# Attention and retention branch products of a hybrid encoder layer: half-width order, sums on VectorE, other buffer counts and later planner times

## The chip, the cores and the metric

The kernel runs on one core of one Trainium2 chip. The metric is the device time of one execution in microseconds; the kernel before took 1951.42 us in the median of three runs (1950.37 to 1952.2).

## What is computed

One layer of a streaming encoder, for a prompt of 2048 frames and a sample of 64 frames, in fp32:

```python
h = rmsnorm(x, norm_g) @ w_in                 # 10 groups of columns
qa, ka, va, za, qb, kb, vb, zb, ga, gb = split(h)
oa = diff_attention(qa, ka, va)               # 4 heads of 128
ob = retention(qb, kb, vb)                    # 4 heads of 128
oa = rmsnorm(oa, subln_g) * (1 - lam_init) * silu(za)
ob = rmsnorm(ob) * silu(zb)
m = sigmoid(ga + b_gate[0]) * (oa @ w_oa) + sigmoid(gb + b_gate[1]) * (ob @ w_ob)
y = x + m @ w_out                             # w_oa, w_ob: 512 x 1024, w_out: 1024 x 1024
```

Keys, values and the retention state are outputs too. The change touches the lines from `silu` to `m`, and the loads of the last product.

## The kernel before, in words

Each fp32 operand of a product is split into a high and a low part, and each product is three matmuls (high by high, high by low, low by high). The first and longest part of the program is the input projection (the matmuls of L587) with attention and retention between. Its results, the gates and the branch outputs among them, are kept transposed in DRAM (`zaT`, `zbT`, `gaT`, `gbT`, `oaT`, `obT`). The last two stages are of interest here; they are called the **merge stage** and the **y stage**.

**The merge stage** makes `m`, transposed, in 8 groups of 264 columns (256 prompt frames and 8 sample frames). `out_stream` (L2085) loops over group `g`, branch `br` (0 attention, 1 retention) and 8 column tiles `ct` of 128 channels. `m_tile` (L1797) issues the 12 matmuls of one tile (4 tiles of the contraction by 3, L1816 to L1818) into one PSUM bank. There are eight banks (`mm`, `s` and `at` twice each, `pv`, `tp`), and tile `ct` always gets the same kind of bank, so TensorE can be eight tiles ahead of the bank that has to be emptied next. `m_fin` (L1826) empties it: VectorE multiplies the bank by the gate, in place in the gate's tile (L1831). After branch 0 the result waits in `gm`; after branch 1 GpSimd adds the two (L1842, into a tile `mo`), copies the 8 sample columns aside (L1843, `msf`), and the sum is stored to DRAM (`mT`).

Three chains feed this. `out_prep` (L1709) loads a pair of tiles `on` and `z` (both with tag `oz`, 6 buffers) for each group, branch and half of the contraction; `og_fin` (L1752) multiplies them on GpSimd (L1756), takes the sigmoid of `z` on ScalarE (L1759), multiplies again on VectorE (L1762), and splits the result on ScalarE (L1770, `ogh`) and VectorE (L1773, `ogl`) into tiles with tag `og` (8 buffers: one group). `gate_prep` (L1787) loads the gates in pairs of column tiles, branch 0 into tag `ga` (4 buffers) and branch 1 into tag `gb` (3 buffers), and `gate` (L1778) takes their sigmoid on ScalarE (L1784). `load_wout` (L1642) and `wout_unit` (L1665) prepare `w_out` in the background: loads into `wst` tiles, and work on GpSimd, ScalarE and VectorE (L1669 to L1689).

**The y stage** multiplies `m` by `w_out` with seven block products per group (`y_quad`, L1915; matmuls L1941 to L1943). `y_load` (L1739) loads the four blocks of a group back from `mT` into four `oz` tiles (even groups) or four `ga` tiles (odd ones); `y_sums` and `y_split` (L1854, L1888) form and split the operands.

**What sets the order.** All of these are Python generators run by a planner (`loop`, L92) that keeps a clock for each engine. A step is written out when the planner's TensorE clock has reached the time that the step has asked for. `P`, `A`, `V`, `G` (L125 to L139) charge matmuls, ScalarE, VectorE and GpSimd work; `ld` (L141) issues a load and returns the time at which it is taken to have landed, `nbytes / 300` ns plus `DMA_LAT` (2600 ns); `give(tag, t)` (L122) counts a buffer as free from time `t`, and `take` (L109) waits for that time. The planner's times only set the order of the instructions in each engine's queue. On the chip each engine, and SyncE, which issues every DMA, works its own queue strictly in order, and waits at its head until the semaphores of that instruction have come.

Of the kernel before, what the change touches and what calls it, by code (L numbers as in the profile page):

```python
# [26 lines left out]
GW = 264  # L27
# [39 lines left out]
class Hybrid:  # L67
# [1597 lines left out]
    def wout_unit(self, st, t, dst):  # L1665
        nc = self.nc
        b1, b2, tt = st
        yield t
        nc.gpsimd.tensor_sub(tt[:, 0], b1[:, 1], b1[:, 0])  # L1669
        self.G(256, self.pe)  # L1670
        nc.gpsimd.tensor_sub(tt[:, 1], b2[:, 1], tt[:, 0])
        t1 = self.G(256)
        for d, s in ((dst[0], b1[:, 0:1]), (dst[1], b2[:, 0:1]), (dst[2], tt), (dst[3], b1)):
            n = 256 * s.shape[1]
            if d is dst[2]:
                yield t1
# [5 lines left out]
            nc.scalar.copy(d[0], s)  # L1682
            t = self.A(n, self.pe)
            if d is dst[3]:
                nc.gpsimd.tensor_sub(d[1], s, d[0].bitcast(F32))
                t = self.G(n, t)
            else:
                yield t
                nc.vector.tensor_sub(d[1], s, d[0].bitcast(F32))  # L1689
# [19 lines left out]
    def out_prep(self):  # L1709
        pa = self.z3  # L1710
        for br, name in enumerate(("w_o_diff", "w_o_ret")):
            for kp in range(2):
                h, l = (self.z3w.tile([128, 2, 1024], F32R, tag=f"{name}{n}{kp}", name=f"{name}{n}{kp}") for n in "hl")
                self.wo[br].append((h, l, {}))
        yield from self.load_wo(0)
        for g in range(8):
            gsl = slice(GW * g, GW * g + GW)
            for br, (oT, zT) in enumerate(((self.oaT, self.zaT), (self.obT, self.zbT))):
                for kp in range(2):
                    yield from self.take("oz", 2)  # L1720
# [6 lines left out]
                    self.ogs.append(og)  # L1727
# [6 lines left out]
        yield lambda: all(self.ogs)  # L1734
        for g in range(8):
            yield lambda: len(self.ma) > g
            yield from self.y_sums(g, *self.ma[g])

    def y_load(self):  # L1739
        for g in range(8):  # L1740
            yield lambda: self.mleft[g] == 0 and (self.gated if g % 2 else len(self.ogs) == 32)
            tag, pool = ("ga", self.z4) if g % 2 else ("oz", self.z3)
            yield from self.take(tag, 4)
            a = []
            for ab in range(2):
                for kh in range(2):
                    a.append(self.sb(pool, [128, 2 * GW], tag, "ma")[:, :512])
                    t = self.ld(a[-1].rearrange("p (c t) -> p c t", c=4), self.mT[g, ab, :, 4 * kh:4 * kh + 4, :],
                                1 << 18)
            self.ma.append((a, t, tag))  # L1750

    def og_fin(self, on, z, t, og):  # L1752
        nc = self.nc
        n = 2 * GW
        yield t
        nc.gpsimd.tensor_mul(on, on, z)  # L1756
        t = self.G(n, self.pe)
# [5 lines left out]
        t = self.V(n + 100, t)  # L1763
        self.give("oz", t)
        yield from self.take("og", 2)
# [8 lines left out]
        t = self.V(n + 100, t)  # L1774
        self.give("oz", t)
        og.append((h, l, t))

    def gate(self, g, br, cp, pair):  # L1778
        t = self.ld(pair, (self.gaT, self.gbT)[br][2 * cp:2 * cp + 2, :, GW * g:GW * g + GW]
                    .rearrange("c p n -> p c n"), 270000)  # L1780
        yield t
        for u in range(2):
            ct = 2 * cp + u
            self.nc.scalar.activation(pair[:, u], pair[:, u], AF.Sigmoid, bias=self.bg[:, br, ct:ct + 1])  # L1784
# [11 lines left out]

    def m_tile(self, g, br, ct, og):  # L1797
        nc = self.nc
        csl = slice(128 * ct, 128 * ct + 128)
        tag = ("mm", "s", "at", "mm", "s", "at", "pv", "tp")[ct]  # L1800
        yield from self.take(tag)
        ps = self.psum(tag)[:, :GW]
        for kt in range(4):
# [3 lines left out]
            ready = tw[ct // 2]  # L1807
            if ct == 0 and u == 0:
                k = 4 * g + 2 * br + kp
                yield lambda: len(self.ogs) > k and self.ogs[k]  # L1810
                og.append(self.ogs[k][0])
                ready = max(ready, og[-1][2])
# [6 lines left out]
            for _ in range(3):  # L1819
                t = self.P(GW)  # L1820
        if ct == 7:
            self.give("og", t, 4)
        self.spawn(self.m_fin(g, br, ct, ps, tag, t), 0)
        yield self.pe

    def m_fin(self, g, br, ct, ps, tag, t):  # L1826
        nc = self.nc
# [5 lines left out]
        self.give(tag, t)  # L1833
        if br == 0:
# [5 lines left out]
        yield max(t, t2)  # L1840
        m = self.sb(self.z4, [128, GW], "mo")
        nc.gpsimd.tensor_add(m, a, gs)  # L1842
        nc.gpsimd.tensor_copy(self.msf[:, ct, 8 * g:8 * g + 8], m[:, 256:GW])  # L1843
# [10 lines left out]
    def y_sums(self, g, a, t, tag):  # L1854

# [11 lines left out]
        t3 = self.G(512, t)  # L1867
        self.give(tag, t3)
        yield t
# [7 lines left out]
        t = yield from self.y_split(g, a21)  # L1877
        self.give(tag, t)
        t = yield from self.y_split(g, a12)
        self.give(tag, max(t, t4))  # L1880
        t = yield from self.y_split(g, a22)
        self.give(tag, t)
        if t4 > self.pe:
# [150 lines left out]
    def sample_split(self):  # L2034
        nc = self.nc
        yield lambda: sum(self.mleft) == 0
        yield self.pool + LAT
        h, l = (self.ms[:, :, k] for k in range(2))
        nc.scalar.copy(h, self.msf)
        t = self.A(512, self.pe)  # L2040
        yield t
        nc.vector.tensor_sub(l, self.msf, h.bitcast(F32))
        self.msn.append(self.V(612, t))

    def y_sample(self):
        nc = self.nc
        yield lambda: self.msn and all(len(w) == 4 for w in self.wlast.values())
        yield max(self.msn[0], *(max(w.values()) for w in self.wlast.values()))
        run = []
# [35 lines left out]
    def out_stream(self):  # L2085
        self.spawn(self.gate_prep(), 0)
        self.spawn(self.load_wout(), 2)
        for g in range(8):
            for br in range(2):
                og = []  # L2090
                for ct in range(8):
                    yield from self.m_tile(g, br, ct, og)
        self.z3x.close()
# [75 lines left out]
    def z_stream(self):  # L2169
# [28 lines left out]
        self.z3w = self.z3x.enter_context(self.tc.tile_pool(name="p3w", bufs=1, side="right"))  # L2198
        self.ogs = []
        self.wo = [[], []]  # L2200
        self.spawn(self.out_prep(), 1)

    def run(self):
# [16 lines left out]
        self.gts = {}  # L2220
        self.msn = []
        self.wout_left = 8
# [90 lines left out]
```

## Time and profile before

| what | value |
|---|---|
| median of three runs | 1951.42 us |
| the profiled execution's own time | 1950.76 us |
| its span in the trace | 1948.9 us |
| granted TensorE clock, mean | 0.995 |
| TensorE busy in the span | 1925.5 us |
| VectorE, ScalarE, GpSimd busy | 1085.8, 1005.5, 530.8 us |

Busy times are sums over the instructions of an engine; on TensorE, matmuls overlap, so a window is full when its busy time equals its length. The granted clock is the share of full speed that TensorE was given. "Idle before" is the time an engine stood still ahead of a group of instructions, with what ended it. A wait "A <- B" means that an instruction of A was released last by one of B.

### The profile page before, as it was taken

To read this page: it belongs to the slowest core of one execution; us is meant where nothing else is said; L and a number is where in the kernel's file an instruction comes from. 1 tells how busy PE (TensorE), PEld (TensorE's weight loads), DVE (VectorE), ACT (ScalarE), POOL (GpSimd) and SP (SyncE) were. 2 spreads that over 40 slices of the span, in tenths; PEclk is the share of its full clock that TensorE was granted. 3 is DMA by queue.
4 is the path that set the end of the run, shared out by engine and by line. 5 is a ranking of instruction groups with operands and counts; after the bars stand their busy time and mean duration, and the time that the engine had idled before them with its cause. 6 is when DMAs were issued, how large, how long until landed. Compare 5 with 4: busy or idle time off the path is not lost.

```text
span 1948.9 us, 32905 instructions
## 1 busy us (share of the span) xinstructions
PE 1925.5 (99%) x11614; PEld 1713.8 (88%) x11614; DVE 1085.8 (56%) x2665; ACT 1005.5 (52%) x2137; POOL 530.8 (27%) x493
## 2 busy tenths in 40 slices
PE   9999999999999999999999999999999999989999
PEld 7878899999889999999988888888888899988787
DVE  6553565636545345638746646646653336646664
ACT  6442676645454535536657656645754435543221
POOL 2320121212121223211112121121112538765442
PEclk9999999999999999999999999999999999999999
DMA  7647464336665868554243242453244656677542
GB/s 246 211 141 195 137 173 127 108 94 170 171 178 161 245 185 233 169 177 149 93 133 117 88 137 92 128 167 98 66 122 134 218 170 205 203 240 224 194 156 77
DMA packets 356198, 308.49 MB, mean 158 GB/s; under 512 B 65729, under 2 KB 313537, under 8 KB 356034
## 3 DMA queue, kind: packets, MB, share of 16 engines
q1 hardware_dynamic: 356034, 306.39, 53.2%
q8 instruction: 92, 1.51, 0.3%
q14 instruction: 72, 0.59, 0.1%
HBM read 201.38 MB, written 99.88 MB: 155 GB/s over the span
## 4 chain that ended last, share of the span: by engine, by line
PE 91%; DMA 3%; POOL 3%; DVE 1%; issue 1%; ACT 1%; SPq 0%; POOLq 0%; ACTq 0%; DVEq 0%
PE mm L587 55%; PE s L1061 3%; PE s L1062 3%; PE at L1169 3%; PE pv L1149 2%; PE pv L1148 2%; PE pv L1147 2%; PE s L1941 1%; PE s L1942 1%; PE s L1943 1%; DMA on<-oaT 1%; PE pv L1528 1%; PE at L1518 1%; PE at L1943 1%; PE tp L784 1%
## 5 line engine op out<-in xcount | busy, mean ns | idle before, releaser
L587 PE MATMUL mm<-xh,wh 128*128 128x512 f32 (+2 forms) x1280 | 457.5, 357 | 0.0
L587 PE MATMUL mm<-xh,wl 128*128 128x512 f32 (+2 forms) x1280 | 452.4, 353 | 0.0
L587 PE MATMUL mm<-xl,wh 128*128 128x512 f32 (+2 forms) x1280 | 451.9, 353 | 0.0
L551 POOL TENSOR_TENSOR wl<-ws,wh 128x512 fp32r<-128x512 f32 x189 | 253.8, 1357 | 671.4 <-ACT wh L541 517.3
L587 PEld LDWEIGHTS mm<-xh,wl 128*128 128x128 f32 x1280 | 240.9, 188 | 31.2
L587 PEld LDWEIGHTS mm<-xh,wh 128*128 128x128 f32 x1280 | 241.3, 189 | 29.0
L587 PEld LDWEIGHTS mm<-xl,wh 128*128 128x128 f32 x1280 | 241.3, 189 | 28.8
L587 PE MATMUL mm<-wh,xh 128*128 128x256 f32 (+1 forms) x696 | 235.9, 339 | 0.5 <-ACT raw L749 0.3
L587 PE MATMUL mm<-wh,xl 128*128 128x256 f32 (+1 forms) x696 | 231.2, 332 | 0.0
L587 PE MATMUL mm<-wl,xh 128*128 128x256 f32 (+1 forms) x696 | 230.7, 331 | 0.0
L1184 DVE TENSOR_TENSOR atl<-at,ath 128x512 fp32r<-128x512 f32 (+1 forms) x144 | 93.0, 659 | 146.5 <-ACT ath L1182 146.5
L887 ACT COPY ev<-mm 128x512 f32<-128x512 f32 x140 | 71.4, 510 | 187.1 <-PE mm L587 164.1
L1100 ACT ACTIVATE row<-row,a_mx 128x1024 f32<-128x1024 f32 (+7 forms) x160 | 153.9, 963 | 5.0 <-DVE a_mx L1080 5.0
L1070 DVE CUSTOM_DVE_ANT_0 row<-s,dfar 128x512 f32<-128x512 f32 (+2 forms) x192 | 117.9, 630 | 58.5 <-PE s L1062 58.2
L587 PEld LDWEIGHTS mm<-wh,xh 128*128 128x128 f32 x696 | 131.9, 190 | 14.1 <-ACT raw L749 0.8
L587 PEld LDWEIGHTS mm<-wh,xl 128*128 128x128 f32 x696 | 131.8, 189 | 13.3
L587 PEld LDWEIGHTS mm<-wl,xh 128*128 128x128 f32 x696 | 132.0, 190 | 12.8
L541 ACT CAST wh<-ws 128x512 fp32r<-128x512 f32 x192 | 115.2, 617 | 47.3 <-PE mm L587 23.5
L950 POOL TENSOR_TENSOR r_y<-r_y,r_sq 128x256 f32<-128x256 f32 x33 | 25.8, 783 | 415.6 <-DVE r_sq L947 143.4
L1182 ACT CAST ath<-at 128x512 fp32r<-128x512 f32 (+1 forms) x144 | 78.5, 565 | 100.0 <-PE at L1169 96.9
L1061 PE MATMUL s<-K,q 128*128 128x512 f32 (+3 forms) x320 | 119.4, 377 | 0.0
L1062 PE MATMUL s<-K,q 128*128 128x512 f32 (+3 forms) x320 | 115.6, 363 | 0.0
(383 smaller groups left out, 4210.6 us busy)
## 6 DMA issues: line engine op xcount, KB each, us to landing
ws<-in_w_in_dram SPq DMA_DIRECT2D x192, 256.0 KB, 3.2
q<-qT SPq DMA_DIRECT2D x128, 128.0 KB, 3.0
V<-vN SPq DMA_DIRECT2D x24, 512.0 KB, 5.6
K<-kT SPq DMA_DIRECT2D x48, 256.0 KB, 4.1
ga<-gaT SPq DMA_DIRECT2D x32, 264.0 KB, 4.1
gb<-gbT SPq DMA_DIRECT2D x32, 264.0 KB, 4.6
xt<-in_x_prompt_dram SPq DMA_DIRECT2D x16, 512.0 KB, 6.0
kn<-in_cache_k_T_dram SPq DMA_DIRECT2D x32, 256.0 KB, 3.4
```

What stands on the lines that cost most here:

```text
L541: self.nc.scalar.copy(h, st)
L551: self.nc.gpsimd.tensor_sub(l, st, h.bitcast(F32))
L587: nc.tensor.matmul(ps, p, q, start=c == 0 and i == 0, stop=c == KC - 1 and i == 2)
L887: nc.scalar.copy(ev, ps)
L1061: nc.tensor.matmul(ps, q1s, kk, start=True, stop=False)
L1062: nc.tensor.matmul(ps, q2s, kk, start=False, stop=True)
L1070: nc.vector.tensor_tensor_reduce(out=units[k0 // 1024][:, k0 % 1024:k0 % 1024 + n], in0=ps, in1=tab, scale=-SLOPES[h], scalar=3.0e38, op0= ...
L1100: nc.scalar.activation(u, u, AF.Exp, bias=mx, scale=-1.0, accum_out=lp[:, k:k + 1])
L1147: nc.tensor.matmul(o, v0, ah[:, s0:s0 + n], start=kt == 0, stop=False)
L1169: nc.tensor.transpose(at[:, w:w + 128], src, self.ident)
L1182: nc.scalar.copy(ah[:, :w], at[:, :w])
L1184: nc.vector.tensor_sub(al[:, :w], at[:, :w], ah[:, :w].bitcast(F32))
```

## The change

- **Half-width order.** A group is now run as four quarters of four column tiles, from a table `HALVES`: for even groups branch 0 on tiles 0 to 3, branch 1 on tiles 0 to 3, branch 1 on tiles 4 to 7, branch 0 on tiles 4 to 7; for odd groups with the branches exchanged. The branch that is first on a half puts its gates into `ga` tiles, the second into `gb` tiles, and the sum is made after the second. The `og` tiles of a branch are given back after its second quarter. Banks go round by a running count, no longer by column tile.
- **Sums on VectorE.** The sum of the branches and the copy of the sample columns move from GpSimd to VectorE.
- **Buffers.** `oz` has 7 tiles instead of 6, `ga` 3 instead of 4. For the y stage an odd group's blocks go to three `ga` tiles and one `gb` tile, each taken by itself, and a group's loads now also wait until two operands of the group ahead are split.
- **Later times in the planner.** A new `LATE` (1000 ns) is added when `oz`, `wst`, `ga`, `gb` tiles are given back and before a sum is stored; a new `LAND` (2000 ns) is added to the time from which loaded `on`, `z` and gate tiles may be used.
- `sample_split` no longer waits for the count of finished sums but uses the time of the last one.

Core of the diff:

```diff
-        "oz": 6, "og": 8, "ga": 4, "gb": 3, "wst": 4, "mo": 4, "xr": 8, "cap": 6}
+        "oz": 7, "og": 8, "ga": 3, "gb": 3, "wst": 4, "mo": 4, "xr": 8, "cap": 6}
...
+LATE = 1000.0
+LAND = 2000.0
...
+HALVES = [[(a, 0, 0), (b, 0, 1), (b, 1, 0), (a, 1, 1)] for a, b in ((0, 1), (1, 0))]
...
-        self.give("wst", t, 3)
+        self.give("wst", t + LATE, 3)
...
-            for br, (oT, zT) in enumerate(((self.oaT, self.zaT), (self.obT, self.zbT))):
+            for br in (0, 1) if g % 2 == 0 else (1, 0):
+                oT, zT = ((self.oaT, self.zaT), (self.obT, self.zbT))[br]
...
     def y_load(self):
         for g in range(8):
...
+            yield lambda: g == 0 or len(self.ya[g - 1]) > 1
+            tags = ("ga", "ga", "ga", "gb") if g % 2 else ("oz",) * 4
...
     def og_fin(self, on, z, t, og):
...
-        yield t
+        yield t + LAND
         nc.gpsimd.tensor_mul(on, on, z)
...
-        self.give("oz", t)
+        self.give("oz", t + LATE)
...
     def gate(self, g, br, cp, pair):
...
-        yield t
+        yield t + LAND
...
     def gate_prep(self):
         for g in range(8):
-            for br in range(2):
-                for cp in range(4):
-                    tag = ("ga", "gb")[br]
+            for br, half, second in HALVES[g % 2]:
+                for cp in range(2 * half, 2 * half + 2):
+                    tag = ("ga", "gb")[second]
                     yield from self.take(tag)
...
-        tag = ("mm", "s", "at", "mm", "s", "at", "pv", "tp")[ct]
+        self.nbank += 1
+        tag = ("mm", "s", "at", "mm", "s", "at", "pv", "tp")[self.nbank % 8]
...
-        nc.gpsimd.tensor_add(m, a, gs)
-        nc.gpsimd.tensor_copy(self.msf[:, ct, 8 * g:8 * g + 8], m[:, 256:GW])
-        t = self.G(GW, t)
-        t2 = self.G(40)
+        nc.vector.tensor_add(m, a, gs)
+        t = self.V(GW, t)
+        nc.vector.tensor_copy(self.msf[:, ct, 8 * g:8 * g + 8], m[:, 256:GW])
+        self.msn = self.V(20)
         if ct % 2:
-            self.give("ga", t + SLACK)
-            self.give("gb", t + SLACK)
-        yield t2 + 2000
+            self.give("ga", t + LATE)
+            self.give("gb", t + LATE)
+        yield t + LATE
...
         for g in range(8):
-            for br in range(2):
-                og = []
-                for ct in range(8):
-                    yield from self.m_tile(g, br, ct, og)
+            ogs = [[], []]
+            for k, (br, half, second) in enumerate(HALVES[g % 2]):
+                for ct in range(4 * half, 4 * half + 4):
+                    yield from self.m_tile(g, br, ct, second, ogs[br])
+                if k > 1:
+                    self.give("og", self.pe + LAT, 4)
```

New lines push the code down: what was L1756, L1831, L1842 and L1843 is L1762, L1835, L1847 and L1849 in the changed kernel, and L1669 to L1685 are L1674 to L1690.

GpSimd's queue in the merge stage before, at the end of group 0: the sums and copies (`mo`, `msf`), the work on `w_out` (`wst`, `wt43l`) and a product for a later group (`on`) stand in one line.

```order
L1842 TENSOR_TENSOR mo<-ga,gb 128x264
L1843 COPY msf<-mo 128x8
L1842 TENSOR_TENSOR mo<-ga,gb 128x264
L1843 COPY msf<-mo 128x8
L1756 TENSOR_TENSOR on<-on,z 128x528
L1678 TENSOR_TENSOR wst<-wst 128x256
L1685 TENSOR_TENSOR wt43l<-wst,wt43h 128x2x256
```

A stretch of the same queue, early in the merge stage of the changed kernel:

```order
L1674 TENSOR_TENSOR wst<-wst 128x256
L1676 TENSOR_TENSOR wst<-wst 128x256
L1685 TENSOR_TENSOR wst<-wst 128x256
L1762 TENSOR_TENSOR on<-on,z 128x528
L1683 TENSOR_TENSOR wst<-wst 128x256
L1690 TENSOR_TENSOR wt43l<-wst,wt43h 128x2x256
```

The sums and copies are gone from this queue; the products `on` now follow only work on `w_out`.

VectorE's queue before, over the second branch of group 0 (products of banks and gates, with work on `w_out` and the low parts `ogl` between):

```order
L1831 TENSOR_TENSOR gb<-mm,gb 128x264
L1773 TENSOR_TENSOR ogl<-on,ogh 128x528
L1689 TENSOR_TENSOR wb21l<-wst,wb21h 128x256
L1831 TENSOR_TENSOR gb<-s,gb 128x264
L1689 TENSOR_TENSOR wt12l<-wst,wt12h 128x2x256
L1831 TENSOR_TENSOR gb<-at,gb 128x264
L1831 TENSOR_TENSOR gb<-mm,gb 128x264
L1831 TENSOR_TENSOR gb<-s,gb 128x264
L1831 TENSOR_TENSOR gb<-at,gb 128x264
L1831 TENSOR_TENSOR gb<-pv,gb 128x264
L1831 TENSOR_TENSOR gb<-tp,gb 128x264
L1762 TENSOR_TENSOR on<-on,z 128x528
```

VectorE's queue in the changed kernel, over the last quarter of group 0:

```order
L1779 TENSOR_TENSOR ogl<-on,ogh 128x528 x2
L1835 TENSOR_TENSOR gb<-at,gb 128x264
L1835 TENSOR_TENSOR gb<-pv,gb 128x264
L1847 TENSOR_TENSOR mo<-ga,gb 128x264
L1849 COPY msf<-mo 128x8
L1847 TENSOR_TENSOR mo<-ga,gb 128x264
L1849 COPY msf<-mo 128x8
L1835 TENSOR_TENSOR gb<-tp,gb 128x264
L1847 TENSOR_TENSOR mo<-ga,gb 128x264
L1849 COPY msf<-mo 128x8
```

Each product of a second branch is now followed, at once or one product later, by its sum and its copy in the same queue.

More of the change, by code (lines that the diff above doesn't have):

```diff
@@ L1733, in out_prep @@
         self.spawn(self.y_load(), 1)
-        yield lambda: all(self.ogs)
+        yield lambda: all(self.ogs.values())
         for g in range(8):
@@ L1740, in y_load @@
         for g in range(8):
-            yield lambda: self.mleft[g] == 0 and (self.gated if g % 2 else len(self.ogs) == 32)
-            tag, pool = ("ga", self.z4) if g % 2 else ("oz", self.z3)
-            yield from self.take(tag, 4)
+            yield lambda: self.mleft[g] == 0 and (self.gated if g % 2 else self.oput == 32)
+            yield lambda: g == 0 or len(self.ya[g - 1]) > 1
+            tags = ("ga", "ga", "ga", "gb") if g % 2 else ("oz",) * 4
             a = []
[L1745 to L1750, printed above, removed]
+            for k, tag in enumerate(tags):
+                yield from self.take(tag)
+                a.append(self.sb(self.z4 if g % 2 else self.z3, [128, 2 * GW], tag, "ma")[:, :512])
+                kh = 4 * (k % 2)
+                t = self.ld(a[-1].rearrange("p (c t) -> p c t", c=4), self.mT[g, k // 2, :, kh:kh + 4, :], 1 << 18)
+            self.ma.append((a, t, tags))
     def og_fin(self, on, z, t, og):
@@ L1774, in og_fin @@
         t = self.V(n + 100, t)
-        self.give("oz", t)
+        self.give("oz", t + LATE)
         og.append((h, l, t))
@@ L1807, in m_tile @@
             ready = tw[ct // 2]
[L1808 to L1811, printed above, removed]
+            if u == 0 and len(og) == kp:
+                yield lambda: self.ogs[g, br, kp]
+                og.append(self.ogs[g, br, kp][0])
                 ready = max(ready, og[-1][2])
@@ L1820, in m_tile, with m_fin @@
                 t = self.P(GW)
-        if ct == 7:
-            self.give("og", t, 4)
-        self.spawn(self.m_fin(g, br, ct, ps, tag, t), 0)
+        self.spawn(self.m_fin(g, br, ct, second, ps, tag, t), 0)
         yield self.pe
-    def m_fin(self, g, br, ct, ps, tag, t):
+    def m_fin(self, g, br, ct, second, ps, tag, t):
         nc = self.nc
@@ L1833, in m_fin @@
         self.give(tag, t)
-        if br == 0:
+        if not second:
             self.gm[ct] = (gs, t)
@@ L1867, in y_sums @@
         t3 = self.G(512, t)
-        self.give(tag, t3)
+        self.give(tags[0], t3)
         yield t
@@ L1877, in y_sums @@
         t = yield from self.y_split(g, a21)
-        self.give(tag, t)
+        self.give(tags[2], t)
         t = yield from self.y_split(g, a12)
-        self.give(tag, max(t, t4))
+        self.give(tags[1], max(t, t4))
         t = yield from self.y_split(g, a22)
-        self.give(tag, t)
+        self.give(tags[3], t)
         if t4 > self.pe:
@@ L2035, in sample_split @@
         nc = self.nc
-        yield lambda: sum(self.mleft) == 0
-        yield self.pool + LAT
         h, l = (self.ms[:, :, k] for k in range(2))
         nc.scalar.copy(h, self.msf)
-        t = self.A(512, self.pe)
+        t = self.A(512, max(self.pe, self.msn))
         yield t
         nc.vector.tensor_sub(l, self.msf, h.bitcast(F32))
-        self.msn.append(self.V(612, t))
+        self.t_ms = self.V(612, t)
     def y_sample(self):
         nc = self.nc
-        yield lambda: self.msn and all(len(w) == 4 for w in self.wlast.values())
-        yield max(self.msn[0], *(max(w.values()) for w in self.wlast.values()))
+        yield lambda: all(len(w) == 4 for w in self.wlast.values())
+        yield max(self.t_ms, *(max(w.values()) for w in self.wlast.values()))
         run = []
@@ L2198, in z_stream @@
         self.z3w = self.z3x.enter_context(self.tc.tile_pool(name="p3w", bufs=1, side="right"))
-        self.ogs = []
+        self.ogs = {(g, br, kp): [] for g in range(8) for br in range(2) for kp in range(2)}
+        self.oput = 0
         self.wo = [[], []]
```

14 lines of the change are left out of this document (8 added, 6 removed).

## The prediction

> **What bounds the kernel now.** First the busy time in windows over the whole span, to find where TensorE is not full.
>
> ```profile
> 0.00:1400.00 1400.00, 1394.37 (x8464) 1242.30 (x8465) 797.67 (x2180) 780.94 (x1690) 271.78 (x223) 1.00 0.53 152
> 1600.00:1650.00 50.00, 45.45 (x350) 45.24 (x349) 29.76 (x54) 24.43 (x53) 37.30 (x46) 0.93 0.72 218
> 1700.00:1750.00 50.00, 45.98 (x354) 45.65 (x353) 24.70 (x46) 20.81 (x44) 31.63 (x43) 0.93 0.78 233
> 1850.00:1900.00 50.00, 50.00 (x217) 40.46 (x216) 31.77 (x42) 12.66 (x21) 21.25 (x13) 1.00 0.46 152
> ```
>
> The columns are the window, its length, the busy time of TensorE, its weight loads, VectorE, ScalarE and GpSimd, the granted clock, the DMA share and GB/s. TensorE is full at full clock outside the merge stage, so only that stage can give much. Next its borders and the length of a tile, from TensorE's timeline (first matmul of the first two tiles, of the last two, and of the y stage), and the stage as one window.
>
> ```profile
> 1571.80 0.28 PE L1816 MATMUL mm<-ogh,w_o_diffh 128*128 128x264 f32 x1
> 1573.25 0.28 PE L1816 MATMUL s<-ogh,w_o_diffh 128*128 128x264 f32 x1
> ...
> 1776.14 0.28 PE L1816 MATMUL pv<-ogh,w_o_reth 128*128 128x264 f32 x1
> ...
> 1777.61 0.28 PE L1816 MATMUL tp<-ogh,w_o_reth 128*128 128x264 f32 x1
> ...
> 1779.09 0.40 PE L1941 MATMUL mm<-wb11h,mh 128*128 128x512 f32 x1
> ...
> 1571.80:1779.10 207.30, 194.80 (x1538) 193.23 (x1537) 113.66 (x203) 98.69 (x212) 136.25 (x177) 0.97 0.70 209
> ```
>
> The stage lasts 207.3 us. A tile that waits for nothing takes 1.45 us (1571.80 to 1573.25) to 1.47 us (1776.14 to 1777.61), and the 128 tiles 185.6 to 188.2 us; I take 187. The stage therefore loses about 20 us: 12.5 us of idle TensorE (207.30 less 194.80), and the rest to a lower clock, 0.97 in the mean (0.03 x 207 is 6 us). Windows of 5 us show where the clock falls.
>
> ```profile
> 1640.00:1645.00 5.00, 1.22 (x5) 1.22 (x6) 4.66 (x8) 5.00 (x12) 3.80 (x5) 0.81 0.84 257
> 1645.00:1650.00 5.00, 5.00 (x25) 5.00 (x24) 1.72 (x5) 1.20 (x3) 4.94 (x6) 0.51 0.43 129
> 1710.00:1715.00 5.00, 2.61 (x12) 2.61 (x13) 3.47 (x8) 3.70 (x8) 3.27 (x5) 0.64 0.96 283
> 1715.00:1720.00 5.00, 5.00 (x31) 5.00 (x31) 1.95 (x3) 2.08 (x4) 4.20 (x7) 0.68 0.95 280
> 1750.00:1755.00 5.00, 3.20 (x27) 2.99 (x26) 2.71 (x4) 3.64 (x8) 3.56 (x4) 1.00 0.25 73
> ```
>
> Then the waits of TensorE, which name what ends them.
>
> ```profile
> PE pv L1816 <- DVE ga L1831: 4.6, 1, 4.6
> PE pv L1816 <- DVE gb L1831: 3.9, 1, 3.9
> ...
> PE tp L1816 <- DVE ga L1831: 1.8, 1, 1.8
> PE mm L1817 <- DVE ogl L1773: 1.1, 1, 1.1
> ...
> PE mm L1816 <- ACT ogh L1770: 1.0, 1, 1.0
> ...
> PE at L1943 <- DVE ml L1896: 0.6, 2, 0.4
> PE at L1941 <- ACT mh L1893: 0.4, 1, 0.4
> ```
>
> Two waits of 4.6 and 3.9 us, and one of 1.8, are for a bank that VectorE has not emptied although TensorE was eight tiles (11.6 us) ahead; 2.1 us are for operands, and 1.0 us falls into the y stage. The two long ones are followed by the slow clock, the 1.8 us one (at 1750) is not. VectorE is not short of time (113.66 of 207.3 us). What held it is seen in the waits of the other engines around the second long stall, in their sums for the stage, and in SyncE's timeline.
>
> ```profile
> ACT z L1759 <- POOL on L1756: 8.5, 2, 7.0
> DVE on L1762 <- ACT z L1759: 7.0, 2, 4.9
> ...
> SPq L142 <- POOL mo L1842: 20.8, 12, 3.7
> SPq L142 <- POOL msf L1843: 16.1, 10, 4.0
> ...
> SPq L142 <- POOL wt43l L1685: 14.3, 4, 6.5
> ...
> 1693.74 10.06 SPq L142 DMA_DIRECT2D wst<-in_w_out_dram  x3
> ```
>
> It is one ring. SyncE stood for most of 10 us at loads of `w_out` tiles that GpSimd had not freed; the loads of `on` and of gates lay behind; GpSimd's next product waited for its load, ScalarE's sigmoid of `z` for GpSimd (7.0 us), VectorE's product for that (4.9 us), and the products that empty the banks stood behind it. The bound of this stage is queues that stand at an instruction written out too early.
>
> **The change, part by part.** The rows with the prices:
>
> ```profile
> ga<-gaT SPq DMA_DIRECT2D x32, 264.0 KB, 4.1
> gb<-gbT SPq DMA_DIRECT2D x32, 264.0 KB, 4.6
> ...
> L1773 DVE TENSOR_TENSOR ogl<-on,ogh 128x528 fp32r<-128x528 f32 x28 | 28.8, 1057 | 2.3 <-ACT ogh L1770 2.3
> L1831 DVE TENSOR_TENSOR ga<-s,ga 128x264 f32<-128x264 f32 x16 | 6.8, 426 | 10.8 <-ACT ga L1784 10.8
> L1689 DVE TENSOR_TENSOR wb21l<-wst,wb21h 128x256 fp32r<-128x256 f32 x8 | 6.1, 764 | 0.5 <-ACT wb21h L1682 0.5
> ...
> L1784 ACT ACTIVATE ga<-ga,bg 128x264 f32<-128x264 f32 x64 | 29.2, 507 | 33.9 <-DMA ga<-gaT 33.9
> ...
> L1770 ACT CAST ogh<-on 128x528 fp32r<-128x528 f32 x28 | 16.3, 625 | 1.8 <-issue 1.8
> ...
> L1842 POOL TENSOR_TENSOR mo<-ga,gb 128x264 f32<-128x264 f32 x57 | 48.7, 855 | 6.4 <-DMA mT<-mo 3.4 <-DVE gb L1831 3.1
> L1843 POOL COPY msf<-mo 128x8 f32<-128x8 f32 x56 | 20.2, 360 | 3.0
> ...
> L245 DVE TENSOR_TENSOR sm_t<-sm_t,ms x51: 155/166/1224, 81.0 to 1489.0; 128x8 f32<-128x8 f32 x32, 128x4 f32<-128x4 f32 x16, 64x8 f32<-64x8 f32 x2, 64x4 f32<-64x4 f32 x1
> ```
>
> *Later planner times.* The planner took a gate pair as landed after 270000/300 + 2600 = 3500 ns; the rows say 4.1 and 4.6 us. With `LAND` it counts 5.5 us, above both medians, so sigmoids and products of `on` stand later in the queues than their data arrive. `LATE` does the same for freed buffers, and so for SyncE. These edits add no instruction. What they cost is lead: about 3 us of the time between a buffer's release and its use.
>
> *Sums off GpSimd.* GpSimd loses 48.7 + 20.2 us of its 136.25 and keeps 67. SyncE's waits for sums and copies (20.8 and 16.1 us) then hang on VectorE. VectorE gains 64 sums and 64 copies. No row has a sum there. From below, a sum costs 0.42 us (the 264-wide product from a bank); from above 0.76 us (the 256-wide difference of two SBUF tiles while GpSimd works); a copy about 0.17 us (the smallest operations). That is 38 to 60 us, or 151 to 173 us busy in a stage of 187. I take the lower half, about 45, since GpSimd does half as much. It lies in VectorE's idle time; if that cover went, each us above 187 would be a us of the stage.
>
> Here the Trainium skill has a rule that speaks against the move: "GPSIMD Engine Reference", section 1 (Specifications), says that GpSimd shares its SBUF interfaces with VectorE and contends with VectorE instructions that have two SBUF inputs. The added sums are of that kind. The rows agree: `ogl` with two SBUF inputs averages 1057 ns, far above twice the 426 ns of the half as wide product from a bank. By the rule all sums would take the upper price; the stage would still fit.
>
> *Half-width order, three `ga` tiles.* A half (two branches on four tiles) is 8 tiles, 11.6 us. With three tiles, the gates of a half's second first-branch pair need the tile of the half before that its second branch frees in its middle. From that release the ring is: SyncE up to 1 us (estimate), landing 4.6, two sigmoids 1.0, two products 0.85, two products of the second branch 0.85, two sums and copies 1.2: 9.5 us. It fits into 11.6 us with 2 us to spare, and eight banks lend another 11.6 us once. Before, the ring with four tiles had a whole group (23.3 us) for about the same work. So this edit frees SBUF for a seventh `oz` tile at the price of a tighter ring. It is the part that I trust least.
>
> *Operands.* A branch's `og` tiles come free a quarter (5.8 us) before the next group needs them, where it was half a group (11.6 us). Two casts and two low parts take 1.25 + 2.1 us by the rows, which fits. I leave the 2.1 us of operand waits in the sum.
>
> *The y stage.* Its products are the same, at the same rate. Only its first operands change place; their tiles come free in the last quarter, 5.8 us ahead, and each product takes longer than its split. I cost it at nothing; the bounds are its 1.0 us of waits gone or doubled.
>
> **Sum.** Against the profiled execution's 1950.76 us: less 20.4 us (207.3 to 187), plus 2.1 us of operand waits, plus 1.8 us for one short bank wait of the kind seen at 1750, gives 1934. Its own time is 0.66 us below the median of the runs shown, so I give 1935. Lower bound: the whole loss goes and tiles run at 1.45 us, 1951.4 less 21.7 (207.3 to 185.6), less 1 us in the y stage: 1929.
>
> For the clock, "TensorE: Matmul & The Clock Gate", part 1, of the Trainium skill says that the clock is halved after an idle window of about 3.4 us and comes back after as much busy time. That agrees with the rows: 0.51 to 0.81 after the long stalls, 1.00 after the 1.8 us one. By the rule two such recoveries cost about 3.4 us together; the windows give 6 to 8, which I use.
>
> **The rivals.**
>
> *Half the stalls stay* (the stage loses 8 to 14 us): the queues still meet transfers that land late, since the landing times are medians and the DMA share reaches 0.95 in the rows around 1715. Against it: GpSimd no longer carries sums, which is the first link of the ring. With 11 of the 20.4 us left the time is 1951.4 less 9.4, 1942.
>
> *The three-tile gate ring paces the stage* (slower). Place: loads of `ga` in the middle of each half. Point: the ring above 11.6 us. Two low parts (2.1 us) queued on VectorE within the ring would bring 9.5 to just 11.6; one late landing on top passes it. Over 16 halves each us above costs 15 us, less the 11.6 us that the banks lend. It turns slower than before at (20.4 + 11.6)/15 = 2.1 us above, 13.7 us; at 14.5 us it gives about 1962. Against it: low parts do not fall into every ring, and VectorE's queue puts the products of the first branch together.
>
> *The stalls only move*: the later planner times stretch the rings as much as they unblock the queues, and the time stays within 0.2% (4 us, about what a measurement of this kernel can tell): 1950.
>
> **How the numbers follow.** The forecast (1929 to 1938) has 0.70. Half the stalls stay: 0.16. The stalls move: 0.05. The gate ring: 0.09. Faster by over 0.2% has 0.86, the same 0.05, slower 0.09. The range reaches from 1929 over the forecast and the second case to 1946.
>
> **What would show it.** Right: the merge stage at 187 to 191 us, granted clock 1.00 throughout it, no wait of TensorE over 2 us, GpSimd near 67 us in the stage and VectorE at 150 to 165, and SyncE's waits for `mo` and `msf` gone or short. Wrong: waits of TensorE's bank for VectorE while VectorE waits for `ga` sigmoids and these for DMA (the gate ring), VectorE above 175 us with sums near 0.76 us, waits on `ogh` at the start of quarters, or a later first product of the y stage.

## The result, and the profile after

The changed kernel takes 1929.8 us (median of four runs, 1929.18 to 1930.79) against 1951.81 us before (four runs, 1950.37 to 1952.23). The ratio is 0.9889, 95% interval 0.9876 to 0.9901: faster by 1.1%, 22 us. The profiled execution took 1930.18 us, with a span of 1928.4 us.

First the borders of the merge stage, from TensorE's timeline, and the stage and two stretches of the y stage as windows (columns as in the prediction's first fence).

```profile
1572.21 0.28 PE L1822 MATMUL s<-ogh,w_o_diffh 128*128 128x264 f32 x1
...
1760.44 0.39 PE L1946 MATMUL mm<-wb11h,mh 128*128 128x512 f32 x1
```

```profile
1572.20:1760.44 188.24, 187.66 (x1537) 187.33 (x1536) 158.22 (x330) 99.72 (x215) 73.77 (x63) 1.00 0.80 237
1760.00:1800.00 40.00, 40.00 (x176) 32.42 (x176) 34.21 (x47) 14.77 (x26) 17.79 (x11) 1.00 0.75 244
1800.00:1900.00 100.00, 100.00 (x431) 80.28 (x430) 59.14 (x78) 24.90 (x42) 40.12 (x26) 1.00 0.46 146
```

The stage lasts 188.2 us, 19.1 less than before. TensorE idles 0.6 us in it instead of 12.5, and the granted clock is 1.00 throughout. The rest, from the first y product to the end of the span, takes 168.0 us (1928.4 less 1760.44) where it took 169.8. The stage began 0.4 us later. Together that is 20.5 us, the difference of the two spans (1948.9 and 1928.4). These are the waits of TensorE and then of SyncE in the stage, and the groups of VectorE and of GpSimd. Line 147 is a load, line 152 a store (142 and 147 before).

```profile
PE at L1823 <- DVE ogl L1779: 0.6, 1, 0.6
```

```profile
SPq L152 <- DVE msf L1849: 41.4, 32, 7.5
SPq L147 <- DVE ogl L1779: 13.0, 13, 3.4
SPq L147 <- DVE mo L1847: 7.9, 7, 2.1
SPq L152 <- DVE mo L1847: 7.7, 10, 1.7
...
SPq L147 <- POOL wt43l L1690: 6.4, 4, 2.2
```

```profile
L1847 DVE TENSOR_TENSOR mo<-ga,gb 128x264 f32<-128x264 f32 x62 | 35.5, 572 | 0.9
L1779 DVE TENSOR_TENSOR ogl<-on,ogh 128x528 fp32r<-128x528 f32 x28 | 22.3, 826 | 0.1
...
L1849 DVE COPY msf<-mo 128x8 f32<-128x8 f32 x62 | 19.9, 320 | 2.1
...
L1762 POOL TENSOR_TENSOR on<-on,z 128x528 f32<-128x528 f32 x22 | 31.6, 1438 | 37.6 <-DMA on<-oaT 13.2 <-DVE ga L1835 10.4 <-DMA on<-obT 8.8
```

No bank wait is left. SyncE still stands, but elsewhere. Before, its loads stood 97.7 us in all, 36.9 of them for GpSimd's sums and copies; now they stand 49.5 us, 7.9 of them for VectorE's sums. Its stores stood 23.6 us and now stand 58.1, 49.1 of them for VectorE's sums and copies. Loads that lie behind a standing store are late by that much, and still TensorE has what it needs: idle time of SyncE shows trouble only when what lies behind it is wanted.

### The profile page after: what moved, and what is told of

Read it like the earlier page. It is cut to its first block, busy times and chain, and to the rows that moved or that the text cites. A ratio compares the mean times of both kernels' runs of the same rounds, so it can differ in the third digit from the quotient of the medians.

```text
span 1928.4 us, 32898 instructions
## 1 busy us (share of the span) xinstructions
PE 1918.3 (99%) x11614; PEld 1708.6 (89%) x11614; DVE 1133.9 (59%) x2793; ACT 1004.4 (52%) x2137; POOL 459.2 (24%) x365
## 4 chain that ended last, share of the span: by engine, by line
PE 95%; DVE 2%; DMA 1%; ACT 1%; issue 0%; POOL 0%; SPq 0%; DVEq 0%; ACTq 0%; POOLq 0%
PE mm L592 55%; PE s L1066 3%; PE s L1067 3%; PE at L1174 3%; PE pv L1154 2%; PE pv L1153 2%; PE pv L1152 2%; PE s L1946 1%; PE s L1948 1%; PE s L1947 1%; PE pv L1533 1%; PE at L1523 1%; PE tp L789 1%; PE at L1946 1%; PE at L1948 1%; PE mm L1946 1%
## 5 line engine op out<-in xcount | busy, mean ns | idle before, releaser
L592 PEld LDWEIGHTS mm<-xl,wh 128*128 128x128 f32 x1280 | 241.3, 189 | 28.7
L1075 DVE CUSTOM_DVE_ANT_0 row<-s,dfar 128x512 f32<-128x512 f32 (+2 forms) x192 | 118.0, 630 | 58.3 <-PE s L1067 58.1
L546 ACT CAST wh<-ws 128x512 fp32r<-128x512 f32 x192 | 115.2, 617 | 49.1 <-PE mm L592 23.1
```

Of the source, the lines that this page charges most:

```text
L546: self.nc.scalar.copy(h, st)
L592: nc.tensor.matmul(ps, p, q, start=c == 0 and i == 0, stop=c == KC - 1 and i == 2)
L1075: nc.vector.tensor_tensor_reduce(out=units[k0 // 1024][:, k0 % 1024:k0 % 1024 + n], in0=ps, in1=tab, scale=-SLOPES[h], scalar=3.0e38, op0= ...
```

## The experiments

Two theories. **Times**: the queues stood because instructions were written out too early, and `LAND` and `LATE` cured that. This is where the prediction put its weight. **Sums**: GpSimd, in whose queue the sums lay among its products, was the link of the ring that could not keep up, and moving the sums cured it. A rival to both is the half-width order, as a gain or as a tight ring. Each part was undone in the changed kernel, and each put alone into the kernel before. Ratios are to the kernel before, timed on the same chip. The stage is from the first `ogh` product to the first y product.

### Sums back on GpSimd

```diff
-        nc.vector.tensor_add(m, a, gs)
-        t = self.V(GW, t)
-        nc.vector.tensor_copy(self.msf[:, ct, 8 * g:8 * g + 8], m[:, 256:GW])
-        self.msn = self.V(20)
+        nc.gpsimd.tensor_add(m, a, gs)
+        t = self.G(GW, t)
+        nc.gpsimd.tensor_copy(self.msf[:, ct, 8 * g:8 * g + 8], m[:, 256:GW])
+        self.msn = self.G(40)
```

> The changed kernel with one part undone: the sums and the copies of the sample columns run on GpSimd again. Theory 1 (planner times: the stalls came from instructions written out before their data had landed) expects little: 1930 to 1935 us, merge stage under 193 us, GpSimd near 140 us busy in it. Theory 2 (GpSimd's queue was the link that closed the ring) expects most of the stalls back: 1942 to 1952 us, with waits of TensorE's banks of 2 us and more. Theory 3 (the half-width order is what gives the room) expects 1930 to 1935 us.

Measured: 1963.97 us, ratio 1.0056 (1.0041 to 1.0071), so slower than the kernel before, and above what any of the three theories gave. The stage lasts 223.5 us. TensorE's waits in the stage, SyncE's, and windows over the longest of them:

```profile
PE mm L1822 <- DVE ga L1835: 27.9, 5, 17.5
```

```profile
SPq L152 <- POOL mo L1847: 61.3, 26, 7.9
SPq L152 <- POOL msf L1849: 48.7, 28, 6.9
```

```profile
1571.40:1794.90 223.50, 194.84 (x1537) 193.51 (x1536) 116.81 (x206) 99.99 (x215) 139.53 (x187) 0.93 0.66 199
1650.00:1655.00 5.00, 0.92 (x8) 0.70 (x6) 3.98 (x5) 1.62 (x5) 4.94 (x6) 1.00 0.52 150
1655.00:1660.00 5.00, 0.00 (x0) 0.00 (x0) 1.25 (x1) 0.48 (x1) 2.62 (x5) 0.54 0.67 193
1660.00:1665.00 5.00, 0.00 (x0) 0.00 (x0) 0.00 (x0) 0.00 (x0) 0.19 (x1) 0.50 1.04 350
```

Between 1660 and 1665 all five engines all but stand, and the DMA is at its peak. The timelines of SyncE, GpSimd, ScalarE, VectorE and TensorE give the chain, in this order:

```profile
1642.86 1.22 SPq L147 DMA_DIRECT2D wst<-in_w_out_dram  x2
1648.98 0.37 SPq L152 DMA_DIRECT2D mT<-mo  x1
...
1653.65 0.36 SPq L152 DMA_DIRECT2D mT<-mo  x1
...
1659.55 0.42 SPq L147 DMA_DIRECT2D on<-oaT  x1
...
1664.81 1.29 POOL L1762 TENSOR_TENSOR on<-on,z 128x528 f32<-128x528 f32 x1 [7.06 <-DMA on<-oaT]
1666.07 0.72 POOL L1683 TENSOR_TENSOR wst<-wst 128x256 f32<-128x256 f32 x1
...
1666.82 0.62 ACT L1687 CAST wt43h<-wst 128x512 fp32r<-128x512 f32 x1 [11.35 <-POOL wst L1683]
1667.35 0.92 ACT L1790 ACTIVATE ga<-ga,bg 128x264 f32<-128x264 f32 x2
...
1667.89 0.43 DVE L1835 TENSOR_TENSOR ga<-mm,ga 128x264 f32<-128x264 f32 x1 [11.14 <-ACT ga L1790]
...
1668.38 0.59 PE L1822 MATMUL mm<-ogh,w_o_reth 128*128 128x264 f32 x1 [17.46 <-DVE ga L1835]
```

SyncE stood from 1644.1 to 1649 and again to 1653.6 at stores of sums that GpSimd had not made. The load of `on` was therefore issued at 1659.55. GpSimd's product waited 7.06 us for it, with a `w_out` difference behind it. ScalarE stood 11.35 us at the cast of that difference, with the gate sigmoid behind it; VectorE 11.14 us at the product that needs this sigmoid; and TensorE 17.46 us for its bank. It is the prediction's ring with all later planner times in place, closed by the sums on GpSimd. One link differs: there SyncE stood at loads of `w_out` tiles, here at stores of sums and copies (110.0 us in the stage, 61.3 and 48.7).

### Planner times undone, one by one

```diff
-LAND = 2000.0
+LAND = 0.0
```

> The changed kernel with LAND set to 0: loads count as landed after 3.5 us again, the rest stays. Theory 1 expects bank waits of TensorE to come back in part: 1935 to 1945 us, with ScalarE waiting for gate loads ahead of other work. Theories 2 and 3 expect no change: 1929 to 1932 us.

Measured: 1931.93 us, ratio 0.9892 (0.9877 to 0.9907), stage 188.9 us. Nothing lost that can be measured. For `LATE`, the `ga` and `gb` tiles again come free at `SLACK` (400), and a sum's store keeps its 1000 ns:

```diff
-LATE = 1000.0
+LATE = 0.0
-            self.give("ga", t + LATE)
-            self.give("gb", t + LATE)
-        yield t + LATE
+            self.give("ga", t + SLACK)
+            self.give("gb", t + SLACK)
+        yield t + 1000.0
```

> The changed kernel with LATE set to 0 (gate tiles given back 400 ns after the sum, as before), LAND and the rest kept. Theory 1 expects SyncE to stand longer at loads whose tile is not free: 1932 to 1940 us. Theories 2 and 3 expect no change: 1929 to 1932 us.

Measured: 1929.85 us, ratio 0.9886 (0.9869 to 0.9902), stage 188.0 us. Nothing either.

### Full-width order kept

```diff
-HALVES = [[(a, 0, 0), (b, 0, 1), (b, 1, 0), (a, 1, 1)] for a, b in ((0, 1), (1, 0))]
+HALVES = [[(0, 0, 0), (0, 1, 0), (1, 0, 1), (1, 1, 1)]] * 2
-        "oz": 7, "og": 8, "ga": 3,
+        "oz": 6, "og": 8, "ga": 4,
```

(The branches are also loaded in their old order, and `og` tiles come free after each branch.)

> The changed kernel with the order undone: each group runs branch 0 on all eight column tiles, then branch 1, with four ga tiles and six oz tiles as before; sums on VectorE, LATE and LAND stay. Theory 1 and theory 2 expect little: 1929 to 1934 us. Theory 3 expects most of the stalls back: 1942 to 1952 us. If the half-width order made the gate ring tighter, as the prediction feared, this one is no slower than the changed kernel.

Measured: 1927.78 us, ratio 0.9873 (0.9856 to 0.9889), stage 187.3 us without any wait of TensorE:

```profile
1571.28:1758.58 187.30, 187.30 (x1538) 187.30 (x1537) 160.22 (x331) 99.98 (x215) 77.55 (x65) 1.00 0.79 240
```

So the half-width order brings nothing here; its interval overlaps that of the whole change, so the 2 us between them are not settled.

### Parts alone

Into the kernel before went `LATE` and `LAND` only:

> The kernel before with the later planner times alone (1000 ns on oz, wst, ga, gb tiles given back, 2000 ns on the landing of on, z and gates); order, buffers and sums on GpSimd as before. Theory 1 expects most of the gain: 1931 to 1938 us. Theory 2 (GpSimd) and theory 3 (order) expect 1945 to 1953 us.

Measured: 1953.55 us, ratio 1.001 (1.0001 to 1.0019). The stage is 212.6 us, with 18.2 us of bank waits. The times alone bring nothing. The sums and copies alone:

> The kernel before with the sums and copies on VectorE alone. Theory 2 expects most of the gain: 1931 to 1938 us. Theories 1 and 3 expect little: 1943 to 1953 us, with VectorE's queue standing at products whose sigmoid is late.

Measured: 1935.5 us, ratio 0.9915 (0.9901 to 0.993), 16.6 us of the gain. The half-width order with seven `oz` and three `ga` tiles, and the changed loads of the y stage, with sums on GpSimd and the early planner times:

> The half-width order, seven oz and three ga tiles alone: sums on GpSimd and early planner times as before. Theory 3 expects most of the gain: 1931 to 1938 us. Theories 1 and 2 expect 1943 us or more; the gate ring that the prediction feared would put it above 1952 us.

Measured: 1963.61 us, ratio 1.0057 (1.004 to 1.0074): some 11 us slower than before. In its stage TensorE waits 9.4 us for `ogh`, 0.9 us for `ogl` and 10.2 us for banks. The stage of these two, as windows:

```profile
1571.07:1766.02 194.95, 190.30 (x1537) 189.65 (x1536) 152.80 (x324) 98.30 (x212) 75.45 (x65) 0.98 0.75 227
```

```profile
1571.62:1793.50 221.88, 201.22 (x1537) 197.83 (x1536) 110.07 (x205) 98.64 (x214) 136.58 (x187) 0.94 0.67 200
```

### Both planner times undone together

Undone one by one they cost nothing, and yet the sums alone (0.9915) stayed 0.26%, 5 us, behind the whole change (0.9889). So both went at once: from the changed kernel, and from the one with the full-width order.

> The changed kernel with both planner times of before (LAND 0, buffers counted free early), so that the sums on VectorE and the half-width order stand alone. Each time alone could be undone at no cost. If one covers for the other: 3 to 8 us lost, 1933 to 1938, with waits of SyncE for buffers and TensorE's waits for banks back. If the times are worth nothing in any combination: 1928 to 1932, and what lies between the sums alone (1935.5) and the whole change comes from the other parts.

> The kernel with the full-width order (four ga tiles, six oz tiles) and the sums on VectorE, without the later planner times: what is left of the change beside the sums is the loads of the y stage one tile at a time and the split of the sample columns. If the planner times bring what the sums alone don't (1935.5): about 1935, with the 4.4 us wait of TensorE for a bank. If the y stage's own edits bring it: 1928 to 1930, and the same stage of 188 us in the merge as the changed kernel only by chance.

Measured: 1936.85 us, ratio 0.9923 (0.9906 to 0.994), with the half-width order; 1936.17 us, 0.9923 (0.9905 to 0.9942), with the full width. Each of the two times covers for the other, and the pair is worth 7 to 10 us once the sums are on VectorE (0.34 and 0.50% by the ratios). The y stage's own edits are in the full-width kernel and don't lower its time. With the full width 4.1 us of short bank waits came back, as expected. With the half width it is waits for operands, which was not expected; TensorE's waits there:

```profile
PE at L1823 <- DVE ogl L1779: 5.5, 4, 3.2
PE s L1823 <- DVE ogl L1779: 0.6, 1, 0.6
```

The eight combinations of the three parts, as ratios:

| sums on | order | early times | later times |
|---|---|---|---|
| GpSimd | full | 1 (before) | 1.001 |
| GpSimd | half | 1.0057 | 1.0056 |
| VectorE | full | 0.9915, 0.9923 | 0.9873 |
| VectorE | half | 0.9923 | 0.9889 |

(The two values are without and with the other edits, of the y stage.) The sums decide, the times add to them, and the half-width order costs 0.5 to 0.6% with the sums on GpSimd and nothing that can be told apart otherwise.

### How near VectorE is to its bound

Each sum is made twice, the second time with the same result:

```diff
         self.msn = self.V(20)
+        nc.vector.tensor_add(m, a, gs)
+        t = self.V(GW, t)
```

> The changed kernel with each of the 64 sums made twice (the second writes the same values), which adds about 37 us to VectorE's 157 us in the merge stage (64 times the 574 ns of a sum in the changed kernel's trace). If VectorE's cover ends at the stage's length, as the prediction said, the stage grows from 188 to about 195 to 200 us: 1936 to 1942 us. If queue order alone counts and the load of VectorE does not, 1930 to 1932 us. If the gate ring is near its limit, the added time in each half passes it and it is 1945 us or more.

Measured: 1945.91 us, ratio 0.9966 (0.9953 to 0.9979); the stage is 203.1 us, VectorE busy 185.8 of it. The time lies in the range that was given to the gate ring, above the 1936 to 1942 us for the length of VectorE's work. The trace speaks for VectorE's work all the same. Here is a window over the long middle of the stage, and VectorE's waits for `ga` sigmoids in the whole of it:

```profile
1591.00:1741.00 150.00, 139.26 (x1102) 137.56 (x1102) 145.53 (x290) 76.66 (x163) 65.17 (x56) 0.98 0.75 227
```

```profile
DVE ga L1835 <- ACT ga L1790: 1.8, 2, 1.0
```

VectorE is 97% busy there and waits only 1.8 us for these sigmoids, which a gate ring would have made late. Windows of 20 us of the changed kernel itself show why so little room was left:

```profile
1591.00:1611.00 20.00, 20.00 (x167) 20.00 (x166) 19.25 (x38) 10.72 (x25) 11.04 (x11) 1.00 0.85 253
...
1651.00:1671.00 20.00, 20.00 (x167) 20.00 (x166) 19.62 (x36) 13.30 (x31) 13.68 (x13) 1.00 0.82 249
...
1731.00:1751.00 20.00, 20.00 (x166) 20.00 (x165) 12.60 (x34) 8.41 (x20) 0.00 (x0) 1.00 0.56 164
```

158 of 188 us sounds like slack, but while `w_out` tiles are being split VectorE is 96 to 99% busy; the slack lies in the first 20 us and in the last 50.

### What it is about GpSimd: its place in the ring, or its load

Only the small copies went back:

```diff
-        nc.vector.tensor_copy(self.msf[:, ct, 8 * g:8 * g + 8], m[:, 256:GW])
-        self.msn = self.V(20)
+        nc.gpsimd.tensor_copy(self.msf[:, ct, 8 * g:8 * g + 8], m[:, 256:GW])
+        self.msn = self.G(40, t)
```

> The changed kernel with only the small copies (8 columns) back on GpSimd, and the sums on VectorE. VectorE loses 60 x 0.325 = 19.5 us, GpSimd gains about 21 us. By the in-order queues: each copy makes GpSimd wait for VectorE's sum ahead of its next product, and mo comes free only after it; that is a part of the old ring, so 3 to 15 us lost, 1932 to 1945, with SyncE's waits for msf by GpSimd and TensorE's waits for banks back. If only the amount of work on each engine counts: no loss, 1927 to 1931, since GpSimd with about 95 us and VectorE with about 138 us are both far from 188.

Measured: 1928.6 us, ratio 0.9881 (0.9866 to 0.9896), stage 187.25 us, no wait of TensorE. The waits of GpSimd, then of SyncE:

```profile
POOL msf L1849 <- DVE mo L1847: 26.1, 11, 8.0
```

```profile
SPq L152 <- DVE mo L1847: 27.4, 18, 7.3
SPq L147 <- POOL wt43l L1690: 18.4, 4, 5.6
```

GpSimd stands 26.1 us for VectorE's sums, up to 8.0 us at a time, and that costs nothing: the stores wait for the sum (`DVE mo`), not for the copy. So the expectation of the in-order theory, 3 to 15 us lost, was wrong. GpSimd standing at these copies did no harm here. The other side of the question was put by work that hangs on nothing (a 160-column tile of its own):

```diff
+        nc.gpsimd.tensor_add(self.gx, self.gx, self.gx)
+        nc.gpsimd.tensor_add(self.gx, self.gx, self.gx)
+        self.G(360)
```

> The changed kernel, and behind every sum GpSimd adds a small tile (128x160) of its own to itself twice. Nobody reads it, it waits for nothing, and no DMA hangs on it: about the busy time that the sums and copies had there, without their place in the ring of buffers. If the sums cost the time because each waited for VectorE's products and SyncE's stores and buffers waited for it (in-order queues): no change beyond 5 us, 1928 to 1935, and GpSimd's waits stay short although it is busy some 130 to 150 us in the stage. If they cost it because GpSimd was too busy (its products of branch tiles late) or because it slows VectorE at the shared SBUF interfaces: VectorE's differences of two SBUF tiles back at about 1017 to 1057 ns, and the time back towards the kernel with the sums on GpSimd, 1945 to 1964.

Measured: 1981.59 us, ratio 1.0149 (1.013 to 1.0168); three of its four runs lie between 1979.67 and 1982.67, the fourth took 8727 us, for which no profile was taken. It is not the experiment that was meant. GpSimd's groups between 1575 and 1661, a window of the same kernel, and SyncE's waits from 1600 to 1662:

```profile
L1849 POOL TENSOR_TENSOR gx<-gx 128x160 f32<-128x160 f32 x64 | 31.2, 488 | 4.7
L1848 POOL TENSOR_TENSOR gx<-gx 128x160 f32<-128x160 f32 x64 | 31.1, 486 | 4.5
L1762 POOL TENSOR_TENSOR on<-on,z 128x528 f32<-128x528 f32 x3 | 3.9, 1302 | 0.0
```

```profile
1620.00:1630.00 10.00, 0.00 (x0) 0.00 (x0) 0.00 (x0) 0.00 (x0) 8.81 (x18) 0.57 0.00 0
```

```profile
SPq L147 <- POOL gx L1848: 25.9, 1, 25.9
SPq L147 <- POOL wst L1683: 17.0, 1, 17.0
```

All 128 additions were done in the first 87 us, when only 12 of the sums behind which they were written had been made. So GpSimd's queue does not keep the order of the program text. The kernel says the same: it fixes the order by hand for TensorE, ScalarE and VectorE alone (`manual_schedule` with `MANUAL`, L2230 and L2247 in the kernel before). The stretch of GpSimd's queue shown under "The change" has L1685 ahead of L1683, which `wout_unit` writes first. What was said of the planner in "The kernel before, in words", that its times set the order in each engine's queue, therefore holds for these three engines and not for GpSimd; nor does that list name SyncE. Why the additions went ahead is not shown; that they wait for nothing is a likely reason. Only three products of `on` got through among them. SyncE stood 25.9 us at a load of a `w_out` tile that GpSimd had not freed, and everything else stood behind that. Around it TensorE's windows are empty and its clock falls to 0.57. It shows that work ahead of GpSimd's products is enough to close the ring, with no link to sums, stores or gates. It says nothing on contention, and since the work was bunched, nothing on how much of the sums' cost was their load and how much their place. It also lays open a third reading: moving the sums to VectorE takes them out of a queue that the planner does not order and puts them into one that it does. No run parts that from the change of engine.

## Why the prediction was right or wrong

**What bounds the kernel: right in place and size, half right in cause.** Of about 20 us lost in the merge stage 19.1 came back, and the ring of SyncE, GpSimd, ScalarE, VectorE was seen again, link by link, when the sums went back. The cause given to it, queues that stand at an instruction written out too early, is only half of it. With the sums on GpSimd later planner times change nothing (1.001, 1.0057 to 1.0056). They add 7 to 10 us only where the sums are on VectorE. The forecast took the whole loss less two small terms, whichever part of the change would bring it back. That its number came out therefore says nothing for the cause that it named, and in this it was lucky. (207.3 less 187 is 20.3 us and not 20.4; nothing hangs on the tenth.)

**Later planner times: a gain, not alone.** The prediction gave them no price of their own and let the parts share the 20.4 us. It did not say that the two times can stand for each other. It also took `LATE` to set SyncE's order, which the kernel does not fix by hand.

**Sums off GpSimd: right, its terms less so.** A sum took 0.572 us in the mean, between the bounds of 0.42 and 0.76, and a copy 0.320 us, where 0.17 was taken. Both means mix two kinds, as VectorE's and then GpSimd's timeline show:

```profile
1642.15 0.98 DVE L1847 TENSOR_TENSOR mo<-ga,gb 128x264 f32<-128x264 f32 x1
...
1643.25 0.42 DVE L1847 TENSOR_TENSOR mo<-ga,gb 128x264 f32<-128x264 f32 x1
```

```profile
1642.11 0.74 POOL L1685 TENSOR_TENSOR wst<-wst 128x256 f32<-128x256 f32 x1
1645.14 1.31 POOL L1762 TENSOR_TENSOR on<-on,z 128x528 f32<-128x528 f32 x1 [2.30 <-DMA on<-oaT]
```

Of the 62 sums in the stage's trace, 37 ran while no GpSimd instruction did and took 0.42 to 0.44 us each; the other 25 overlapped one and took 0.785 us in the mean, up to 1.52. Of the 62 copies, 44 of the 45 that overlapped none took 0.17 us; the 17 others took 0.65 us in the mean. So neither bound is a price for all sums: a sum has the lower one while GpSimd stands and up to three times as much while it works. The products from a bank took 0.41 to 0.43 us either way. This agrees with the rule of the Trainium skill on shared SBUF interfaces ("GPSIMD Engine Reference", section 1, Specifications). The prediction's reading of it, all sums at 0.76 us, does not hold, because GpSimd was busy only 73.8 of 188.2 us. `ogl`, also with two SBUF inputs, fell from 1057 to 826 ns as GpSimd's busy time fell from 136.25 us.

Sums and copies are 55.4 us (35.5 and 19.9), but VectorE's busy time rose by only 44.6 (113.66 to 158.22), the 45 that was taken. Two things make up the difference, each about 5.4 us. The other operations became shorter on balance (`ogl` alone by 6.5 us). And neighbouring instructions overlap more: a window's busy time is not a sum over instructions, though it was called one ahead of the prediction. It counts overlapped time once: VectorE's groups add up to 173.9 us in 158.22 us of busy time (124.0 in 113.66 before). So the 45 came out by luck: the work that was added is 55.4 us. GpSimd was predicted at 67 us and had 73.8. What the prediction missed is that VectorE's cover is not 30 us spread out: in the stretch with the `w_out` splits it is nearly used up, which the doubled sums showed.

**Half-width order: rightly the part trusted least.** The gate ring was reckoned at 9.5 us of 11.6, and it holds with the sums on VectorE, where no bank wait is left. With the sums on GpSimd the kernel with this order is 0.5 to 0.6% slower, as the rival had it. That the three-tile ring does this is not shown. In the chain shown above the late `ga` sigmoid stands behind a cast of a `w_out` tile, and that chain starts at stores of sums; in the run with the order alone 9.4 of 20.5 us of TensorE's waits are for `ogh`, and SyncE stands 78.6 us at stores of GpSimd's sums and copies (18.6 before). The prediction did not state that the cost of the order depends on where the sums are made.

**Operands and the short bank wait:** 2.1 and 1.8 us were kept in the sum; 0.6 and 0 remained. **The y stage** was costed at nothing, within 1 us; the rest of the span became 1.8 us shorter, outside that bound. It is no effect of the edits there: from the first y product to the end of the span the kernel with the times alone, whose y stage is the old one, takes 167.3 us too (1951.0 less 1783.69), and the one with the sums alone 167.4 (1933.4 less 1766.02). The one profile of before, with 1.0 us of waits at the start of that stage, is the exception. These three terms are why 1929.8 lies 5 us below the 1935: 2.7 from the stage (190.9 reckoned, 188.2 measured) and 1.8 from the rest, less 0.4 for its later start, and 1.0 from the offset between profiled run and median, which changed its sign.

**What would show it:** stage and clock came out as said. SyncE's waits for `mo` and `msf` did not go (49.1 us at stores), only the loads' did; a store's wait turned out to be no sign of trouble by itself.

**The rivals.** Half the stalls staying, or only moving, is what the sums alone or the times alone give (1935.5 and 1953.55), not the whole change.

Open stay the load of the sums, their place in GpSimd's queue and the order of that queue against each other, why either planner time covers for the other, and whether the full-width order is faster by 2 us.

## What to carry to other kernels

Ask of each operation in an in-order queue what stands behind it and who waits for its result; here a copy whose result nothing wanted soon stood there for 8 us unharmed, while a sum that stores and buffers hang on did not. Ask also who sets the order of that queue. Undo parts one by one and also together: two edits that each look worthless may cover for each other. Read the room on an engine in the stretch where it is fullest, not in the mean of the stage.

## What the runs showed of the hardware

On VectorE a sum of two SBUF tiles of 264 columns took 0.42 to 0.44 us while no GpSimd instruction ran, and 0.785 us in the mean when it overlapped one; the 8-column copy behind it took 0.17 us in the first case (44 of 45) and 0.65 in the second. A product of the same width from a PSUM bank took 0.41 to 0.43 us in both. The granted clock was 0.54, then 0.50, in the 5 us windows within a wait of 17.5 us, and the merge stage's mean clock fell to 0.93 there. That stage was 36.2 us longer than the one with full-width order and no waits (223.5 and 187.3 us), while its waits came to 28.7 us: long stalls cost more than themselves.
